# First mixer started on half of the features, and a fixed order of the router chain, in a two-block transformer kernel on one core

## The chip, the core and the metric

The kernel runs on one NeuronCore of a Trainium2 chip. The core has a matrix engine (PE; its weight loads are shown apart, as PEld), a vector engine (DVE), a scalar engine (ACT), a general engine (POOL) and a sequencer that issues most transfers (SP). Each takes its instructions in order and they meet at semaphores. The metric is the device time of one execution in microseconds (us): 730.86 us before, the median of three runs (730.46 to 731.74).

## The reference

One sequence of 256 tokens, 1024 features, everything in float32, goes through two blocks. Only the first block's front and its router are touched by the change:

```
mod = silu(c) @ w_ada + b_ada              # 1024 x 6144, cut into six vectors of 1024
h   = rms_norm(x, g_mix) * (1 + scale_m) + shift_m
x   = x + gate_m * hybrid_mixer(h)         # h @ w_in (1024 x 2896), two attentions, w_out
h   = rms_norm(x, g_ffn) * (1 + scale_f) + shift_f
x   = x + gate_f * hierarchical_moe(h)     # 4 groups of 8 experts, 2 chosen per token
```

The second block (a gated recurrence and a dense feed-forward layer) follows on the same x.

## The kernel before

**Tiles.** A feature index is written on 128 partitions times 8: feature 8p + j lies on partition p, in slice j of a tile. `hTh[:, j]` and `hTl[:, j]` (128 x 256 tokens) are the leading and the remaining bits of slice j of h. A weight is cut in the same way (`split`, `hilo`, lines 85 to 93: ACT copies the high part, `wih`, DVE subtracts it, `wil`), and `mm3` makes three products of a pair. `mm` (line 99) issues every product, so nearly all of PE's rows carry the line L100 and are told apart by their tiles.

**Start.** SP loads four pieces of 1 MB of `w_ada` for the shift (vector 0), then x, then four pieces for the scale (vector 1), then `w_in` columns. `ada(v)` multiplies c's silu (`csr`) with the four pieces into one bank (`p_ada`), ACT copies it (`part`), small products turn it into a column (`p_col`) and DVE adds the bias (`modcol`). x is normed into `xn`, PE turns it (`p_tr`), and `scaled` (line 414) makes `hTh` and `hTl` of all eight slices with the factor `ac` = (1 + scale) g_mix. Only then the projections start: `proj_fm` (line 467) works in four steps of two slices, each of 24 products (`p_w`) into two banks.

**The rest of the mixer.** A string of letters (line 885) names the order of the remaining steps: i, q, b, a are the projections for the index queries, the two query sets and the keys, X and Y the index search on DVE, B to E the attentions. A scheduler places what is not pinned by `tc.keep_in_program_order`; `holding` switches that pinning on, its second entry for PE as well.

**Router.** After the mixer the tokens (two halves, t = 0 and 1) go through `square`, `rstd`, `normed`, `logits`, `groups`, `experts`, `rank`, `places`; `gather_t(t)` (line 998) gathers the tokens of the first four experts by a product of `xn2` with a 0/1 tile `P` (`p_xg`). `gather` (line 1059) scales the result into `xg`, `gate_up` runs the experts (`p_gu`). `cut3` (line 1008) splits `xn2` into three bf16 parts for the gathers of the later units; two of its four steps write `xn2` or read it for the last time (L1011, L1013).

**Buffers.** Weights live in rings: 11 buffers of 1 MB (`raw`), five more in `raw2` and five in `raw3` (`RING`, line 29). `xn2` takes one of the five of `raw3`. SP issues loads in order, so a load that waits for its buffer holds up all behind it. The eight units of four experts follow: unit 0 and the last run straight through, units 1 to 6 each end in a branch (`branch`, line 1302) for an overfull expert, and the loads for the buffers of such a unit are issued behind that branch.

Of the kernel before, what the change touches and what calls it, by code (L numbers as in the profile page):

```python
# [16 lines left out]
T = 256  # L17
D = 1024
# [14 lines left out]
def tile_block(ctx: ExitStack, tc: tile.TileContext, A, out):  # L33
# [87 lines left out]
    act.dma_start(gcol[:, 0], dram("g_mix", 0, [[8, 128], [1, 8]]))  # L121

# [9 lines left out]

    def win_load(c0, n):
        return [load_cols(f"win{c0}_{k}", "w_in", WIN, c0, n, 4 * k, 4) for k in range(2)]

# [29 lines left out]
    small_load(w_bf, dram("w_in", 2888, [[8 * WIN, 128], [WIN, 8], [1, 8]]))  # L165
    small_load(gcol[:, 1], dram("g_ffn", 0, [[8, 128], [1, 8]]))
# [29 lines left out]

    w_iq = win_load(768, 512)
    w_ik = load_cols("wik", "w_in", WIN, 1280, 72, 0, 8)
# [4 lines left out]
    w_bq, w_bk, w_bv, w_aq = [], [], [], []  # L203
    later = {"bq": w_bq, "bk": w_bk, "bv": w_bv, "aq": w_aq}
    for v in (2, 3, 5, 4):
        wada[v] = []
    for name in 'bq bq bk 2 2 bk bv bv 3 aq kv 2 2 3 3 aq 3 4 4 4 4 5 5 5 5'.split():
        if name == "kv":
            w_kv = load_cols("wkv", "w_in", WIN, 512, 256, 0, 8)
        elif name in COLS:  # L210
            c0, n = COLS[name]
            k = len(later[name])
            later[name].append(load_cols(f"win{c0}_{k}", "w_in", WIN, c0, n, 4 * k, 4))
        else:
            ada_piece(int(name))
# [112 lines left out]
    def ada(v):  # L328
# [68 lines left out]

    def transpose_block(src, banks, t):
        for j in range(8):
            pe.transpose(banks[j // 2][:, j % 2, t * 128:t * 128 + 128], src[:, j::8], ident)  # L400

    def transposes(src, by_column=False):

        out_ = [bank([128, 2, T], "p_tr") for _ in range(4)]
        if by_column:
            for j in range(8):
                for t in range(2):
                    pe.transpose(out_[j // 2][:, j % 2, t * 128:t * 128 + 128], src[:, t, j::8], ident)
        else:
            for t in range(2):  # L410
                transpose_block(src[:, t], out_, t)
        return out_

    def scaled(banks, scale, bias, hi, lo, keep):

        for j in range(8):
            p = banks[j // 2][:, j % 2]
            sc = scale[:, j:j + 1]
            if bias is None:
                act.activation(hi[:, j], p, AF.Copy, scale=sc)  # L420
                dve.scalar_tensor_tensor(lo[:, j], p, sc, f32(hi[:, j]), op0=OP.mult, op1=OP.subtract)
            else:
                act.activation(hi[:, j], p, AF.Identity, bias=bias[:, j:j + 1], scale=sc)
                full = keep.tile([128, T], FT, name="full", tag="fin", bufs=3)
                dve.tensor_scalar(full, p, sc, bias[:, j:j + 1], op0=OP.mult, op1=OP.add)
                (dve if j % 2 else pool).tensor_tensor(lo[:, j], full, f32(hi[:, j]), op=OP.subtract)

# [3 lines left out]
    xn = prob1.rearrange("p (t a) b -> p t (a b)", t=2)  # L431
    g0, g1 = ada(0), ada(1)
    for _ in g0:
        pass
# [3 lines left out]
    next(g1)  # L438
    xTb = [bank([128, 2, T], "p_tr") for _ in range(4)]
    for t in range(2):  # L440
        transpose_block(xn[:, t], xTb, t)
        next(g1)
    for _ in g1:
        pass
    ac = small.tile([128, 8], FT, name="ac")
    dve.scalar_tensor_tensor(ac, modcol[:, 1], 1.0, gcol[:, 0], op0=OP.add, op1=OP.mult)

# [384 lines left out]

    st = proj_fm(w_iq, iqT, 1.0)
    c0, m0 = next(st)
    r0_ = c0()
    scaled(xTb, ac, modcol[:, 0], hTh, hTl, a1)
    pend.append(lambda: m0(*r0_))
    def loads1():
# [20 lines left out]
    def router_weights():  # L859
# [3 lines left out]
        for j in range(8):  # L863
# [13 lines left out]

    work = {"i": st, "k": proj_ik(), "q": proj_fm(w_bq, bqT, 0.125), "b": proj_fm(w_bk, bkT, 1.0), "v": proj_bv(),
            "a": proj_fm(w_aq, aqT, 0.125, perm=True), "n": proj_kv(), "o": proj_out(0, obT, obL, rsb),
# [63 lines left out]
    def rstd(t, step):  # L943
# [53 lines left out]

    def gather_t(t):
        for j in range(8):
            mm(xgb[j // 4][:, j % 4], xn2[:, t, j::8], P0f[:, t], t == 0 and j % 4 == 0, t == 1)  # L1000

# [5 lines left out]

    def cut3(src, parts):

        act.activation(parts[0], src, AF.Copy)  # L1010
        dve.tensor_tensor(src, src, parts[0], op=OP.subtract)  # L1011
        act.activation(parts[1], src, AF.Copy)
        dve.tensor_tensor(parts[2], src, parts[1], op=OP.subtract)  # L1013

# [305 lines left out]
    for k, st in enumerate(units):  # L1320
        free = 0 < k < nu - 1
        n = len(st.es)
        gate_up(st, "g")
        if not free:
            load_experts(n)
        gate_up(st, "u")
        if not free:
            load_experts(n)
        silu(st)
        if k == 0:  # L1330
            gate_row_end()
        if k == 3:
            fallback()
# [622 lines left out]
```

## Time and profile before

| | |
|---|---|
| median of three runs | 730.86 us |
| the profiled execution, its own time | 731.0 us |
| its span, first to last instruction | 729.3 us |
| PE busy | 661.0 us (91%) |
| PEld, DVE, ACT busy | 511.3, 400.2, 303.5 us |
| read from HBM | 194.81 MB |

The profile is of one execution; all views below are of it. [...] Three stages can be told apart in the page's slices: the mixer up to about 178 us, where PE is 9 tenths busy, the experts from about 200 to 400 us, where the DMA engines are full and PE is not, and the second block, where PE is full to the end.

### The profile page before, as it was taken

How to read it: one execution, taken by the hardware profiler on the slowest of the kernel's cores; microseconds unless marked ns; L12 is line 12 of the kernel's file. 1: busy time of each engine (PE TensorE's matmuls, PEld its weight loads, DVE VectorE, ACT ScalarE, POOL GpSimd, SP SyncE). 2: the span in 40 equal slices, each digit the busy share in tenths (PEclk: the TensorE clock that was granted, in tenths of full speed). 3: DMA queues.
4: the chain of work that ended last, by engine and by line, in shares of the span. 5: the costliest groups of instructions: out<-in, count | busy, mean ns of one | idle time of the engine just before them, and what ended most of it. 6: DMA issues, size and time to landing. Idle time of an engine off the chain costs nothing. (4 is left out here: it accounts for less than half of the span.)

```text
span 729.3 us, 13242 instructions
## 1 busy us (share of the span) xinstructions
PE 661.0 (91%) x5489; PEld 511.3 (70%) x5489; DVE 400.2 (55%) x753; ACT 303.5 (42%) x505; POOL 46.1 (6%) x71
## 2 busy tenths in 40 slices
PE   4799999999899776898696999999999999999996
PEld 1498787677745524445252499987899999898994
DVE  2367967877653221323312378879576555555555
ACT  1446454754541101101110286775465444444445
POOL 7010000001000000000000153100000000000001
PEclk9899999999899998999987999999999999999998
DMA  9999669996469899998999999633535555550001
GB/s 343 372 381 375 233 262 337 378 420 218 175 273 421 328 417 416 359 423 328 421 421 412 372 364 391 220 117 116 174 116 175 196 200 196 172 202 17 1 1 58
DMA packets 69202, 196.93 MB, mean 270 GB/s; under 512 B 7550, under 2 KB 33219, under 8 KB 57350
## 3 DMA queue, kind: packets, MB, share of 16 engines
q1 hardware_dynamic: 67558, 195.30, 70.8%
q8 instruction: 53, 0.87, 0.5%
q10 hardware_dynamic: 1216, 0.30, 0.2%
q0 software_dynamic: 352, 0.28, 0.1%
q14 instruction: 23, 0.19, 0.1%
HBM read 194.81 MB, written 1.05 MB: 269 GB/s over the span
## 5 line engine op out<-in xcount | busy, mean ns | idle before, releaser
L100 PE MATMUL p_gu<-Xl,wguh 128*128 128x256 f32 x352 | 99.8, 284 | 0.0
L100 PE MATMUL p_gu<-Xh,wgul 128*128 128x256 f32 x352 | 99.3, 283 | 0.0
L100 PE MATMUL p_gu<-Xh,wguh 128*128 128x256 f32 x352 | 98.9, 283 | 0.1
L100 PEld LDWEIGHTS p_gu<-Xl,wguh 128*128 128x128 f32 x352 | 67.5, 192 | 0.5
L100 PEld LDWEIGHTS p_gu<-Xh,wguh 128*128 128x128 f32 x352 | 67.1, 192 | 0.7 <-ACT Xh L1385 0.4
L100 PEld LDWEIGHTS p_gu<-Xh,wgul 128*128 128x128 f32 x352 | 67.4, 192 | 0.3 <-DVE wgul L87 0.2
L100 PE MATMUL p_gu<-eg,xg 128*32 128x256 f32 x576 | 43.9, 434 | 16.6 <-PEq L1302 9.2
L100 PEld LDWEIGHTS p_gu<-eg,xg 128*32 128x32 f32 x576 | 21.1, 123 | 37.9 <-issue 26.8
L87 DVE TENSOR_TENSOR wdnl<-wdn,wdnh 128x1024 fp32r<-128x1024 f32 x22 | 27.0, 1225 | 32.4 <-ACT wdnh L86 32.4
L1155 DVE TENSOR_TENSOR sl<-sl,p_gu 128x256 f32<-128x256 f32 x9 | 3.8, 421 | 71.0 <-ACT sl L1154 71.0
L1154 ACT ACTIVATE sl<-p_gu 128x256 f32<-128x256 f32 x9 | 3.5, 383 | 89.4 <-PE p_gu L100 89.4
L100 PE MATMUL p_w<-hTh,wih 128*128 128x256 f32 x128 | 37.7, 298 | 2.5 <-ACT wih L86 2.5
L87 DVE TENSOR_TENSOR wgul<-wup,wguh 128x1024 fp32r<-128x1024 f32 x22 | 27.0, 1225 | 21.3 <-ACT wguh L86 20.2
L86 ACT ACTIVATE wdnh<-wdn 128x1024 fp32r<-128x1024 f32 x22 | 23.3, 1058 | 36.5 <-PE p_gu L100 35.9
L1072 ACT ACTIVATE xg<-p_xg,modcol,af 128x128 f32<-128x128 f32 x36 | 15.5, 460 | 54.1 <-DVE xg L1074 53.8
L87 DVE TENSOR_TENSOR wgul<-wgt,wguh 128x1024 fp32r<-128x1024 f32 x22 | 26.9, 1225 | 19.8 <-ACT wguh L86 19.8
L100 PE MATMUL p_dn<-ed,aT 128*32 128x512 f32 (+2 forms) x304 | 33.1, 573 | 4.9 <-ACT aT L1162 4.9
L100 PE MATMUL p_w<-Xh,w2h 128*128 128x256 f32 x128 | 37.0, 289 | 0.5 <-ACT w2h L86 0.3
L86 ACT ACTIVATE wguh<-wgt 128x1024 fp32r<-128x1024 f32 x22 | 23.3, 1061 | 33.7 <-PE p_gu L100 18.2
L100 PE MATMUL p_w<-hTl,wih 128*128 128x256 f32 x128 | 37.0, 290 | 0.0
L100 PE MATMUL p_w<-hTh,wil 128*128 128x256 f32 x128 | 36.7, 291 | 0.0
L100 PE MATMUL p_w<-Xh,w2l 128*128 128x256 f32 x128 | 36.1, 284 | 0.6 <-DVE w2l L87 0.6
(624 smaller groups left out, 1591.0 us busy)
## 6 DMA issues: line engine op xcount, KB each, us to landing
eg<-in_w_gate_dram SPq DMA_DIRECT2D x32, 1024.0 KB
eu<-in_w_up_dram SPq DMA_DIRECT2D x32, 1024.0 KB
ed<-in_w_down_dram SPq DMA_DIRECT2D x28, 1024.0 KB
wada<-in_w_ada_dram SPq DMA_DIRECT2D x24, 1024.0 KB
w<-in_w_in_dram SPq DMA_DIRECT2D x11, 1024.0 KB
wgt<-in_w_gate_up_dram SPq DMA_DIRECT2D x11, 1024.0 KB
wup<-in_w_gate_up_dram SPq DMA_DIRECT2D x11, 1024.0 KB
wdn<-in_w_down_dram SPq DMA_DIRECT2D x11, 1024.0 KB
```

The source lines that it names most:

```text
L86: held(act.activation(hi, src, AF.Copy))
L87: held(eng.tensor_tensor(lo, src, f32(hi), op=OP.subtract))
L100: held_pe(pe.matmul(o, lhsT, rhs, start=start, stop=stop, skip_group_check=True))
L1072: act.activation(xg[:, j], b[:, jj], AF.Identity, bias=bf_[:, j:j + 1], scale=af[:, j:j + 1])
L1154: act.activation(st.s[:st.n], st.b[:st.n, 0:256], AF.Silu)
L1155: dve.tensor_tensor(st.s[:st.n], st.s[:st.n], st.b[:st.n, 256:512], op=OP.mult)
```

## The change

It does four things.

1. **Features are numbered anew in the first mixer.** Feature 512h + 4p + j is now slice 4h + j, so the first four slices are the first half of the features. The biases and g_mix are loaded to fit (`bcol` in three transfers instead of one).
2. **The start goes by halves.** Pieces of `w_ada` hold 512 columns: two for the first half of the scale, then x, two for the first half of the shift, the first halves of the i and q weights, and only then the four pieces of the second halves. The class `Cols` takes the place of `ada` for vectors 0 and 1. `w_bf` and `wik` become two transfers each.
3. **The order of both halves is pinned on all engines:** two steps of i and one of q on the first four slices, the columns of the second half, one more step of q, the last four slices.
4. **In the router** `normed` writes `xn2` slice by slice, so that `gather_t` and `cut3` read it in one run, and reads `xt` with the stride instead; `cut3` is pinned behind `gather(0)`; `gather_t(0)` is cut in six and two slices around the second half's `rank`; two fillers on PE (`warm`) go; the pinning reaches over the first unit, and `gate_row_end` (`p_row`) goes behind both of its products.

```diff
-    act.dma_start(bcol, dram("b_ada", 0, [[8, 128], [D, 6], [1, 8]]))
+    act.dma_start(bcol[:, 3:5], dram("b_ada", 3 * D, [[8, 128], [D, 2], [1, 8]]))
+    for v in range(2):
+        act.dma_start(bcol[:, v].rearrange("p (h j) -> p h j", h=2),
+                      dram("b_ada", v * D, [[4, 128], [512, 2], [1, 4]]))
...
+    def load_cols(name, c0, n, k=None):
+        src = [dram("w_in", 512 * WIN * h + c0, [[4 * WIN, 128], [WIN, 4], [1, n]]) for h in range(2)]
+        return load(name, (8, n), *src) if k is None else load(name, (4, n), src[k])
...
-    for _ in range(4):
-        ada_piece(0)
+    ada_half(1, 0)
     tc.keep_in_program_order(nc.sync.dma_start(xt, dram("x", 0, [[D, 128], [128 * D, 2], [1, D]])))
-    for _ in range(4):
-        ada_piece(1)
+    ada_half(0, 0)
+    w_iq = [load_cols("win768_0", 768, 512, 0)]
+    w_bq = [load_cols("win1352_0", 1352, 512, 0)]
+    ada_half(1, 1)
+    ada_half(0, 1)
...
+    class Cols:
+        def __init__(self, v, h):
+            self.v, self.h, self.p = v, h, bank([128, 512], "p_ada")
+        def prod(self, q):
+            for r in range(4):
+                mm(self.p[32 * r:32 * r + 32], csr[:, 4 * q + r, :], wada[self.v, self.h][q][:, r], q == 0, q == 1)
+        def cols(self):
+            self.part = a1.tile([128, 512], FT, name="part", tag="fin", bufs=3)
+            held(act.activation(self.part.rearrange("p (j n) -> p j n", j=4),
+                                self.p.rearrange("p (n j) -> p j n", j=4), AF.Copy))
+        def turn(self):
+            v, hs = self.v, slice(4 * self.h, 4 * self.h + 4)
+            p = bank([128, 4], "p_col")
+            for j in range(4):
+                mm(p[:, j:j + 1], self.part[:, 128 * j:128 * j + 128], sel4, j == 0, True)
+            held(dve.tensor_tensor(modcol[:, v, hs], p, bcol[:, v, hs], op=OP.add))
+            if v:
+                held(dve.scalar_tensor_tensor(ac[:, hs], modcol[:, 1, hs], 1.0, gcol[:, 0, hs],
+                                              op0=OP.add, op1=OP.mult))
...
+    def turn_half(h):
+        xTb.extend(bank([128, 2, T], "p_tr") for _ in range(2))
+        for t in range(2):
+            for j in range(4):
+                held_pe(pe.transpose(xTb[2 * h + j // 2][:, j % 2, t * 128:t * 128 + 128],
+                                     xn[:, t, 512 * h + j:512 * h + 512:4], ident))
...
+    first[1].prod(0)
+    turn_half(0)
+    first[1].prod(1)
+    turn_half(1)
+    first[1].cols()
+    first[1].turn()
+    del holding[:]
...
+    holding += [True, True]
+    run = ahead_of(st)
+    tokens(range(2))
+    run()
+    tokens(range(2, 4))
+    for gen in (st, sq_):
+        ahead_of(gen)()
+    second = [Cols(1, 1), Cols(0, 1)]
+    second[0].prod(0)
+    second[0].prod(1)
+    second[0].cols()
+    run = ahead_of(sq_)
+    second[0].turn()
+    second[1].prod(0)
+    second[1].prod(1)
+    second[1].cols()
+    second[1].turn()
+    tokens(range(4, 6))
+    run()
+    tokens(range(6, 8))
+    del holding[:]
...
-    for c in "iiqikqqFqXFXbbYYbbvYTXXF22XY2XYvvYXYXv2BWBa2aaBYBnB3BC33CCCC3BCanB3C!CR4D45D45D45EH45DDDEoHEoEoDEoDEEESZpppp":
+    for c in "iikqFqXFXbbYYbbvYTXXF22XY2XYvvYXYXv2BWBa2aaBYBnB3BC33CCCC3BCanB3C!CR4D45D45D45EH45DDDEoHEoEoDEoDEEESZpppp":
...
+    xnj = xn2.rearrange("p t (j n) -> p t j n", j=8)
     def normed(t):
-        held(act.activation(xn2[:, t], xt[:, t], AF.Copy, scale=rs2[:, t:t + 1]))
+        held(act.activation(xnj[:, t], xt[:, t].rearrange("p (n j) -> p j n", j=8), AF.Copy,
+                            scale=rs2[:, t:t + 1]))
...
-    gather_t(0)
-    warm(2)
+    gather_t(0, range(6))
     groups(1)
     experts(1)
     rank(1)
+    gather_t(0, range(6, 8))
     places(1)
-    warm(0)
-    gather_t(1)
-    del holding[:]
+    gather_t(1, range(8))
...
     gather(0, xgb)
+    for step in range(2):
+        for t in range(2):
+            cut3(xnj[:, t], [xn3[:, i, t] for i in range(3)], step)
+    del holding[:]
...
+        if k == 0:
+            holding += [True, True]
         gate_up(st, "g")
         if not free:
             load_experts(n)
         gate_up(st, "u")
         if not free:
             load_experts(n)
-        silu(st)
         if k == 0:
             gate_row_end()
+            del holding[:]
+        silu(st)
```

**PE at the start.** `p_ada` are the products with `w_ada`, `p_tr` the turned tokens, `p_col` the columns, `p_w` the projections. PE's rows before:

```order
L100 MATMUL p_ada<-wada_3_101,csr 32x512 x4
L100 MATMUL p_col<-selh,part 64x1 x16
L100 MATMUL p_ada<-wada_0_104,csr 32x512 x4
L400 MATMUL p_tr<-ident,prob_94 128x128 x8
L100 MATMUL p_ada<-wada_1_106,csr 32x512 x4
L400 MATMUL p_tr<-ident,prob_94 128x128 x8
L100 MATMUL p_ada<-wada_2_108,csr 32x512 x4
L100 MATMUL p_ada<-wada_3_110,csr 32x512 x4
L100 MATMUL p_col<-selh,part 64x1 x16
L100 MATMUL p_w<-hTh,wih 128x256
```

And now, the first columns and then, behind 72 products `p_w`, the columns of the second half:

```order
L102 MATMUL p_ada<-wada_0_1_104,csr 32x512 x4
L480 MATMUL p_tr<-ident,prob_96 128x128 x8
L102 MATMUL p_col<-sel_215,part 128x1 x4
L102 MATMUL p_w<-hTh,wih 128x256
...
L102 MATMUL p_ada<-wada_1_0_110,csr 32x512 x4
L102 MATMUL p_ada<-wada_1_1_112,csr 32x512 x4
L102 MATMUL p_col<-sel_215,part 128x1 x4
L102 MATMUL p_ada<-wada_1_0_114,csr 32x512 x4
L102 MATMUL p_ada<-wada_1_1_116,csr 32x512 x4
L102 MATMUL p_col<-sel_215,part 128x1 x4
L102 MATMUL p_w<-hTh,wih 128x256
```

The second half's four pieces, their two copies on ACT and their columns stand between PE's 72nd and 73rd product of the mixer; all columns stood ahead of the first.

**DVE at the start.** `full` is a scaled slice, from which `hTl` is made; `wil` the low part of a weight. Before:

```order
L357 TENSOR_TENSOR modcol<-p_col,bcol 128x8
L446 SCALAR_TENSOR_TENSOR ac<-modcol,gcol 128x8
L425 TENSOR_SCALAR full<-p_tr,ac,modcol 128x256
L87 TENSOR_TENSOR wil<-win_0_119,wih 128x1024
L425 TENSOR_SCALAR full<-p_tr,ac,modcol 128x256 x2
```

And now:

```order
L393 TENSOR_TENSOR modcol<-p_col,bcol 128x4
L89 TENSOR_TENSOR wil<-win_0_106,wih 128x1024
L456 TENSOR_SCALAR full<-p_tr,ac,modcol 128x256 x2
L457 TENSOR_TENSOR hTl<-full,hTh 128x256
L456 TENSOR_SCALAR full<-p_tr,ac,modcol 128x256 x2
```

The first weight's low part has moved ahead of the first slice.

**DVE in the router.** `gone` and `selb` mark the chosen experts of the second half of the tokens, `P` is its 0/1 tile, the rows `xn` belong to `cut3`. Before:

```order
L981 MATCH_REPLACE gone<-top_243,le_1897 128x32
L1011 TENSOR_TENSOR xn_1884<-xn_1884,xn_1910 128x8x128
L982 TENSOR_SCALAR selb<-gone 128x32
L990 SCALAR_TENSOR_TENSOR pos_1902<-p_pos,selb 128x32
L1088 COPY counts<-p_cnt 128x32
L991 TENSOR_TENSOR P_1914<-iota_1898,pos_1902 128x128
```

And now, with the place to which `cut3` has gone:

```order
L1057 MATCH_REPLACE gone<-top_250,le_1899 128x32
L1058 TENSOR_SCALAR selb<-gone 128x32
L1066 SCALAR_TENSOR_TENSOR pos_1904<-p_pos,selb 128x32
L1067 TENSOR_TENSOR P_1916<-iota_1900,pos_1904 128x128
...
L1152 TENSOR_SCALAR xg<-p_xg,af,modcol 128x128
L1189 CAST comb_2060<-crest 128x64
L1190 TENSOR_TENSOR comb_2060<-crest,comb_2060 128x64
L1088 TENSOR_TENSOR xn_1886<-xn_1886,xn_1912 128x1024 x2
L1091 TENSOR_TENSOR xn_1912<-xn_1886,xn_1912 128x1024 x2
```

`selb` follows `gone` at once, and all four steps of `cut3` on DVE stand behind the last `xg` of unit 0.

## Rows read from the trace of the kernel before

**Rows 1.** Windows, all engines: us, PE, PEld, DVE, ACT, POOL, PEclk, DMA share, GB/s.

```profile
190.00:205.50 15.50, 11.93 (x95) 8.38 (x98) 11.18 (x22) 7.97 (x13) 0.00 (x0) 0.89 0.01 1
...
239.00:243.50 4.50, 1.43 (x25) 0.97 (x28) 1.18 (x3) 0.00 (x0) 0.00 (x0) 1.00 0.26 67
243.50:300.00 56.50, 43.01 (x472) 24.97 (x465) 13.83 (x30) 5.04 (x14) 1.02 (x2) 0.88 1.01 415
```

**Rows 2.** Waits of SP's queue, 0 to 215 us: total us, times, longest.

```profile
SPq L252 <- DVE xn L1013: 25.1, 1, 25.1
```

**Rows 3.** Timeline of the start: start us, us, engine, line, operation [idle before <-releaser].

```profile
1.75 0.56 ACTq L121 DMA_DIRECT2D gcol<-in_g_mix_dram  x1
...
4.08 0.89 DVE L324 COPY csr<-cs 128x256 f32<-128x256 f32 x1
...
6.17 1.93 PE L100 MATMUL p_ada<-wada,csr 128*32 128x512 f32 x8 [6.17 <-DMA wada<-in_w_ada_dram]
...
14.47 1.94 PE L100 MATMUL p_ada<-wada,csr 128*32 128x512 f32 x8 [0.64 <-DMA wada<-in_w_ada_dram]
...
17.02 1.06 ACT L395 ACTIVATE prob<-xt 128x1024 f32<-128x1024 f32 x1
...
21.91 0.75 DVE L437 TENSOR_SCALAR prob<-xt,rsr 128x1024 f32<-128x1024 f32 x1
...
21.95 1.94 PE L400 MATMUL p_tr<-ident,prob 128*128 128x128 f32 x8 [0.41 <-DVE rsr L390]
...
26.48 1.06 PE L100 MATMUL p_ada<-wada,csr 128*32 128x512 f32 x8
...
29.22 0.60 ACT L351 ACTIVATE part<-p_ada 128x512 f32<-128x512 f32 x1 [8.22 <-PE p_ada L100]
...
31.02 0.17 DVE L357 TENSOR_TENSOR modcol<-p_col,bcol 128x8 f32<-128x8 f32 x1 [8.36 <-PE p_col L100]
...
33.42 1.23 DVE L87 TENSOR_TENSOR wil<-win,wih 128x1024 fp32r<-128x1024 f32 x1 [0.86 <-ACT wih L86]
...
33.82 0.41 PE L100 MATMUL p_w<-hTl,wih 128*128 128x256 f32 x1
```

**Rows 4.** Windows of the tile p_w alone: us, PE, PEld, DVE, ACT, PEclk, DMA.

```profile
36.00:38.50 2.50, 2.50 (x14) 2.50 (x14) 0.00 (x0) 0.00 (x0) 0.50 1.04 377
40.00:42.00 2.00, 2.00 (x19) 2.00 (x18) 0.00 (x0) 0.00 (x0) 1.00 1.07 383
```

**Rows 5.** Timeline of ACT about 50 us.

```profile
49.94 0.60 ACT L494 ACTIVATE iqT<-p_w 128x512 f32<-128x512 f32 x1 [0.86 <-PE p_w L100]
50.54 1.06 ACT L86 ACTIVATE wih<-win 128x1024 fp32r<-128x1024 f32 x1
```

**Rows 6.** Timeline of PE at 161 us.

```profile
160.79 0.95 PE L100 MATMUL p_ssq<-ones,sq 128*128 128x1 f32 x8
```

**Rows 7.** Timeline of DVE in the router.

```profile
189.49 0.18 DVE L981 MATCH_REPLACE8 gone<-top,le 128x32 f32<-128x32 f32 x1
191.52 2.00 DVE L1011 TENSOR_TENSOR xn<-xn,xn 128x1024 f32<-128x1024 f32 x1 [1.85 <-PE p_xg L100]
193.43 0.18 DVE L982 TENSOR_SCALAR selb<-gone 128x32 bf16<-128x32 f32 x1
...
203.24 2.07 DVE L1013 TENSOR_TENSOR xn<-xn,xn 128x1024 bf16<-128x1024 f32 x1 [1.08 <-ACT xn L1012]
```

**Rows 8.** Timeline of PE in the router.

```profile
186.56 0.91 PE L108 MATMUL p_warm<-ones,ident 128*128 128x128 f32 x6
...
194.54 4.17 PE L100 MATMUL p_xg<-P,xn 128*128 128x128 f32 x16 [0.68 <-DVE P L991]
...
199.84 1.98 PE L100 MATMUL p_row<-modrow,ones 128*128 128x512 f32 x4
...
205.78 3.64 PE L100 MATMUL p_gu<-eu,xg 128*32 128x256 f32 x64
209.35 2.85 PE L100 MATMUL p_xg<-Pq,xn 128*128 128x128 bf16 x48
```

More of the change, by code (lines that the diff above doesn't have):

```diff
@@ L131, in tile_block, with ada_half @@
     WIN = 2896
-    def win_load(c0, n):
-        return [load_cols(f"win{c0}_{k}", "w_in", WIN, c0, n, 4 * k, 4) for k in range(2)]
+    def ada_half(v, h):
+        wada[v, h] = [load(f"wada{v}_{h}_{q}", (4, 512), dram("w_ada", 4 * q * 6 * D + v * D + 512 * h,
+                                                              [[8 * 6 * D, 128], [6 * D, 4], [1, 512]]))
+                      for q in range(2)]
     xt = const.tile([128, 2, D], FT, name="xt")
@@ L164, in tile_block @@
     w_bf = const.tile([128, 8, 8], FT, name="w_bf")
-    small_load(w_bf, dram("w_in", 2888, [[8 * WIN, 128], [WIN, 8], [1, 8]]))
+    for h in range(2):
+        small_load(w_bf[:, 4 * h:4 * h + 4], dram("w_in", 512 * WIN * h + 2888, [[4 * WIN, 128], [WIN, 4], [1, 8]]))
     small_load(gcol[:, 1], dram("g_ffn", 0, [[8, 128], [1, 8]]))
@@ L206, in tile_block @@
         wada[v] = []
-    for name in 'bq bq bk 2 2 bk bv bv 3 aq kv 2 2 3 3 aq 3 4 4 4 4 5 5 5 5'.split():
+    for name in 'bq bk 2 2 bk bv bv 3 aq kv 2 2 3 3 aq 3 4 4 4 4 5 5 5 5'.split():
         if name == "kv":
-            w_kv = load_cols("wkv", "w_in", WIN, 512, 256, 0, 8)
+            w_kv = load_cols("wkv", 512, 256)
         elif name in COLS:
@@ L410, in transposes, with scaled @@
             for t in range(2):
-                transpose_block(src[:, t], out_, t)
-        return out_
-    def scaled(banks, scale, bias, hi, lo, keep):
-        for j in range(8):
+                for j in range(8):
+                    pe.transpose(out_[j // 2][:, j % 2, t * 128:t * 128 + 128], src[:, t, j::8], ident)
+        return out_
+    def scaled(banks, scale, bias, hi, lo, js):
+        for j in js:
             p = banks[j // 2][:, j % 2]
             sc = scale[:, j:j + 1]
[L419 to L426, printed above, removed]
-    xn = prob1.rearrange("p (t a) b -> p t (a b)", t=2)
-    g0, g1 = ada(0), ada(1)
-    for _ in g0:
-        pass
+            held(act.activation(hi[:, j], p, AF.Identity, bias=bias[:, j:j + 1], scale=sc))
+            full = a1.tile([128, T], FT, name="full", tag="fin", bufs=3)
+            held(dve.tensor_scalar(full, p, sc, bias[:, j:j + 1], op0=OP.mult, op1=OP.add))
+            held((dve if j % 2 else pool).tensor_tensor(lo[:, j], full, f32(hi[:, j]), op=OP.subtract))
+    xn = prob1.rearrange("p (t a) b -> p t (a b)", t=2)
+    ac = small.tile([128, 8], FT, name="ac")
+    first = [Cols(1, 0), Cols(0, 0)]
+    holding += [True, True]
+    first[0].prod(0)
+    first[0].prod(1)
+    first[0].cols()
+    first[0].turn()
+    del holding[:]
     for t in range(2):
@@ L437, in tile_block @@
         dve.tensor_scalar(xn[:, t], xt[:, t], r, None, op0=OP.mult)
[L438 to L446, printed above, removed]
+    xTb = []
+    def turn_half(h):
[12 more added lines that the diff above has]
+    del holding[:]
     rsa = const.tile([128, 2], FT, name="rsa")
@@ L831, in flush, with tokens, ahead_of @@
             pend.pop(0)()
[L833 to L837, printed above, removed]
+    st, sq_ = proj_fm(w_iq, iqT, 1.0), proj_fm(w_bq, bqT, 0.125)
+    def tokens(js):
+        scaled(xTb, ac, modcol[:, 0], hTh, hTl, js)
+    def ahead_of(gen):
+        cut, prod = next(gen)
+        r = cut()
+        return lambda: prod(*r)
+    holding += [True, True]
+    run = ahead_of(st)
[18 more added lines that the diff above has]
+    del holding[:]
     def loads1():
@@ L996, in tile_block, with gather_t @@
     xgb = [bank([128, 4, 128], "p_xg") for _ in range(2)]
-    def gather_t(t):
-        for j in range(8):
-            mm(xgb[j // 4][:, j % 4], xn2[:, t, j::8], P0f[:, t], t == 0 and j % 4 == 0, t == 1)
+    def gather_t(t, js):
+        for j in js:
+            mm(xgb[j // 4][:, j % 4], xnj[:, t, j], P0f[:, t], t == 0 and j % 4 == 0, t == 1)
     def gather_mm(u, banks, t):
@@ L1006, in gather_mm, with cut3 @@
                    t == 0 and j % 4 == 0 and i == 0, t == 1 and i == 2)
[L1008 to L1013, printed above, removed]
+    def cut3(src, parts, step):
+        if step == 0:
+            held(act.activation(parts[0], src, AF.Copy))
+            held(dve.tensor_tensor(src, src, parts[0], op=OP.subtract))
+        else:
+            held(act.activation(parts[1], src, AF.Copy))
+            held(dve.tensor_tensor(parts[2], src, parts[1], op=OP.subtract))
     holding += [True, True]
```

33 lines of the change are left out of this document (15 added, 18 removed).

## The prediction

> **What bounds the kernel now.** I read the windows first, then what SP's queue waits for, then the timelines of the two places that change. PE is the bound of the mixer, so a start of its products some time earlier is worth that time there, if PE then keeps its pace. After the mixer the order turns round: from 190.0 to 205.5 us the DMA engines are empty (share 0.01), and from 243.5 on they are full at 415 GB/s while PE has idle time [rows 1]. The reader is to see two things: the empty stretch is paid in full by the stage behind it, and SP stood 25.1 us in one wait, for L1013, the last step of `cut3` on DVE, because `xn2` holds the buffer of the next expert load [rows 2]. There is a second, smaller hole, 239.0 to 243.5 at share 0.26: 3.3 us in which the loads behind unit 1's branch are waited for [rows 1].
>
> **The start.** A piece of 1 MB lands every 2.77 us: the first is used at 6.17, the fourth at 14.47 [rows 3]. Today nine pieces stand ahead of the first product. With the change it is five, so the fifth lands at 6.17 + 4 x 2.77 = 17.3 and the eleventh, the last of the second halves, at 33.9. x now comes third, at 11.7; from the first square (17.02) to the end of the norm (21.91 + 0.75) took 5.6 [rows 3], so `xn` is there at 17.4, no later than that piece. Then on PE: the second four of the first eight transposes, half of 1.94 (18.4), the last `p_ada` group at 1.94 (20.3), eight transposes at 1.94 (22.3), during which ACT's 0.60 copy ends, and the columns. These are now 4 products of one column instead of 16 of 64 rows; the nearest row is `p_ssq`, 8 records in 0.95 [rows 6], so 23.2. From `modcol` to the first product with `hTl` it took 31.02 to 33.82, 2.8 [rows 3]; `ac` leaves that path, `wil` with its 1.23 [rows 3] enters it ahead of `full`. I take 2.8 plus half of 1.23, so 26.6: 7.2 us earlier than 33.82. At the pace of 26.48 (1.06 for a `p_ada` group instead of 1.94 [rows 3]) it would be 1.7 less.
>
> This lead is not kept. [...] Before the low stretch PE had stood mostly idle, waiting for columns and `hTl`. The same idle time now stands before 26.6, so I take the same low stretch, 33.82 to 38.5, 4.7 us or 22 products, and 50 more at 0.12: the 72nd is done at 26.6 + 4.7 + 6.0 = 37.3. There PE turns to the second half's columns, which have landed: twice two groups of 1.06, ACT's 0.60 for which PE must wait, and columns of 0.95, 2 x 3.7 = 7.4, to 44.7. All of that lies on PE's path now, where the same work today lies under the landing of the pieces. The fourth step, 24 x 0.12 = 2.9, covers DVE, ACT and POOL on the second half's tokens; the 96th product is done at 47.6. Today: ACT waits for PE at 49.94 until the first bank is complete, which is the 114th product, so the 96th stands at 49.94 - 18 x 0.12 = 47.8 [rows 5]. From both sides: without any low stretch, 24.9 + 8.6 = 33.5, bounded by the eleventh piece's landing, 43.8, a gain of 4.0; with the columns and the fourth step at the lower clock as well (4 x 0.88 + 1.0 + 24 x 0.09), 54.3, a loss of 6.5. The likeliest row is that of the same low stretch (0.2); half of the low stretch saved would give some 1.2 more. I take a gain of 1.0.
>
> Hidden: ACT issues two transfers more ahead of its first function, 0.56 each; `csr` is done at 4.97, and the first piece lands at 6.17 [rows 3], so 1.1 fits into 1.2. The split `w_bf` and `wik` and the later place of all small loads on SP stand behind full DMA queues (share 1.04 to 1.07 [rows 4]), and their users come after 96 products. If a half piece with its shorter runs lands slower, five pieces at 5% cost 0.7. No wait is added ahead of the later projections: each needs a piece that is queued as early as before.
>
> **The router.** Today DVE starts L1011 at 191.52, after PE has read `xn2`, and `selb`, ready since 189.49 + 0.18, runs only at 193.43. PE's gather of the second half starts 1.1 behind `selb`, at 194.54, and takes 4.17. Three more steps of `cut3` stand between the `xg`, and the u products, which need 3.64, end at 205.78 + 3.64; the gather of unit 1 starts at 209.35 [rows 7, 8].
>
> With the change `selb` runs at 189.7 and the gather starts at 190.8. Its 16 records read a weight tile of stride 8 today, 0.25 each; the fillers of the same shape on an unstrided tile took 0.91 for 6, 0.15 each [rows 8]. The changed `xn2` has the unstrided form, so 16 x 0.15 = 2.4, to 193.2 (bound from above: still 4.17, and 0.5 for the two slices left of the first half, 195.5). The g products start there; they need eight `xg` that no `cut3` step interrupts any more, and take the u group's 3.64 plus some 0.2 of waiting, then u 3.64, then `p_row` 1.98 [rows 8], which has lost the gap that hid it: 193.2 + 0.2 + 7.3 + 2.0 = 202.7, bound 205.0. Against 209.35 that is 6.6 earlier, or 4.4.
>
> What is late next is `cut3` itself: behind the last `xg` at about 196, ACT copies (1.06 [rows 5]) and DVE subtractions (1.23 [rows 3], now that the view is unstrided, against 2.00 [rows 7]) alternate: 1.06 + 4 x 1.23 = 6.0, so 202.0, just ahead of unit 1's gather at 202.7. That is also when SP gets `xn2`'s buffer: 203.24 + 2.07 = 205.3 today, so 3.3 earlier. The DMA queue then runs dry 3.3 earlier, at the hole before 243.5, and is filled again when unit 1 is through, 4.4 to 6.6 earlier; the hole of 3.3 us has room for the difference. Behind it the transfers are full, so what unit 1 gains is kept. I take 6.0, near the upper end, since the fillers' row has the same shape and data type; the low end is 3.3, if only the buffer counts.
>
> [...]
>
> **Sum.** 731.0 (the profiled execution; median 730.86) - 1.0 - 6.0 = 724.0 us.
>
> **Rivals.**
> - *The start pays better.* No low stretch on the first products, as after 38.5, when PE stayed at 1.00 [rows 4]; 3.5 to 4 there and 6 in the router: 721. Against it: PE still waits for columns and `hTl` before 26.6, as it did before 33.82.
> - *Only the buffer counts.* The experts follow SP alone, the gain in the router is 3.3 and the start gives 0.2 to 1: 727. For it: 25.1 us of one wait. Against it: the hole at 239 hangs on unit 1, not on SP's first load.
> - *No change*, 730 to 732: the start loses some 3 (columns at the lower clock) and the router gives 3.3.
> - *Slower.* The stop-and-go start never earns the full clock: 72 products at 0.21 (15.1) from 26.6, columns at 2 x (2 x 1.94 + 0.65 + 1.5) = 12.1, the fourth step 5.1, so the 96th at 58.9 instead of 47.8, 11.1 lost against 6.0 won: 736. It decides from the point where the 96th product comes after 53.8. For it: the clock fell today after the same kind of waiting; against it: it rose again within 4.7 us of products in a row.
>
> [...]
>
> **How the numbers follow.** Both parts as reckoned, 721.8 to 726.5: 0.52. The better start, below that: 0.16. Only the buffer, 726.5 to 729.4: 0.16. Within 0.2% (1.5 us, about what a measurement of this kernel can tell from no change): 0.08. Slower: 0.08. Faster is the first three, 0.84. The range of 719.5 to 729.0 leaves out the last two and the far ends of the second and third.
>
> **What would show it.** Right: the first `p_w` between 24 and 27; a low-clock window there; the second half's `p_ada` near 37; the 96th product 0 to 2 us earlier; `selb` right behind `gone`; gather records of 0.15; unit 1's gather some 7 us earlier, of which 1 is the start's; the empty DMA stretch some 3 us shorter and the hole at 239 nearly gone. Wrong: records of 0.25 in the gather (4.4 instead of 6.0); low clock up to the fourth step; SP still waiting for `cut3` past unit 0's products.

## The result, and the profile after

The changed kernel took 722.0 us (median of four runs, 720.95 to 723.37) where the kernel before took 730.66: a ratio of 0.9878, 95% interval 0.9856 to 0.9900. The forecast was 724.0. In a later set of runs (e11 below) the ratio was 0.9872 (0.9845 to 0.9899). The profiled run has a span of 719.3 us, 10.0 less than before. One of the eight executions of e12 below took 1628 us and is left out of its ratio. The sum came out right; how it is made up did not, and that is what the experiments are about.

**The start.** PE's timeline in the changed kernel:

```profile
7.22 1.93 PE L102 MATMUL p_ada<-wada,csr 128*32 128x512 f32 x8 [7.22 <-DVE csr L337]
...
18.95 1.23 PE L102 MATMUL p_ada<-wada,csr 128*32 128x512 f32 x8
...
24.78 0.38 PE L102 MATMUL p_w<-hTl,wih 128*128 128x256 f32 x1 [1.43 <-POOL hTl L457]
34.90 1.92 PE L102 MATMUL p_ada<-wada,csr 128*32 128x512 f32 x16
...
41.28 1.05 PE L102 MATMUL p_col<-sel,part 128*128 128x1 f32 x8 [0.78 <-ACT part L385]
```

The first product with `hTl` stands at 24.78 instead of 33.82 [rows 3]. The second half's columns lie bare on PE's path from 34.90 to 42.3, 7.4 us, as reckoned. The first product waits for `csr` and is 1.05 us late (7.22 against 6.17): ACT's two extra transfers, which put its first step at 3.79 instead of 2.34, were not hidden. At 18.95 PE was still 0.6 us behind the forecast's 18.4; from there on the last group and the transposes behind it ran in 1.23 each instead of the 1.94 that I had assumed, and 24.78 is earlier than the 26.6 of the forecast.

**The router and SP.** DVE, PE and SP's queue in the changed kernel, the places of [rows 7], [rows 8] and [rows 2]:

```profile
187.34 0.18 DVE L1057 MATCH_REPLACE8 gone<-top,le 128x32 f32<-128x32 f32 x1
187.55 0.18 DVE L1058 TENSOR_SCALAR selb<-gone 128x32 bf16<-128x32 f32 x1
...
196.29 2.36 DVE L1091 TENSOR_TENSOR xn<-xn,xn 128x1024 bf16<-128x1024 f32 x2
```

```profile
188.67 2.02 PE L102 MATMUL p_xg<-P,xn 128*128 128x128 f32 x16
190.62 3.66 PE L102 MATMUL p_gu<-eg,xg 128*32 128x256 f32 x64
194.10 3.64 PE L102 MATMUL p_gu<-eu,xg 128*32 128x256 f32 x64
197.66 1.99 PE L102 MATMUL p_row<-modrow,ones 128*128 128x512 f32 x4
199.48 2.84 PE L102 MATMUL p_xg<-Pq,xn 128*128 128x128 bf16 x48
```

```profile
SPq L263 <- DVE xn L1091: 19.0, 1, 19.0
```

`selb` follows `gone` at once; the 16 gather records take 2.02, 0.13 each instead of 0.25; the gather of unit 1 starts at 199.48 instead of 209.35. SP's wait for `xn2`'s buffer is 19.0 instead of 25.1 us, and it goes on at 198.80 instead of 205.46. The windows show what that does to the DMA engines (last columns: the granted clock of PE as a share of its full one, the PEclk of the rows above; DMA share; GB/s); the hole at 239 to 243.5 [rows 1] is gone:

```profile
190.00:200.00 10.00, 10.00 (x149) 5.84 (x148) 7.80 (x18) 8.20 (x12) 0.00 (x0) 1.00 0.09 15
200.00:205.00 5.00, 4.42 (x70) 3.20 (x71) 1.61 (x5) 2.38 (x7) 0.00 (x0) 1.00 0.91 365
205.00:230.00 25.00, 24.00 (x264) 11.81 (x257) 10.49 (x18) 2.44 (x7) 0.00 (x0) 1.00 1.01 421
230.00:240.00 10.00, 6.36 (x84) 4.06 (x83) 0.56 (x3) 0.00 (x0) 0.00 (x0) 0.83 1.01 415
240.00:250.00 10.00, 9.41 (x141) 5.87 (x132) 2.80 (x7) 2.44 (x7) 0.00 (x0) 1.00 1.01 419
```

### The profile page after: what moved, and what is told of

The parts are those of the page before. It is cut to its first block, busy times and chain, and to the rows that moved or that the text cites. A ratio compares the mean times of both kernels' runs of the same rounds, so it can differ in the third digit from the quotient of the medians.

```text
span 719.3 us, 13181 instructions
## 1 busy us (share of the span) xinstructions
PE 655.8 (91%) x5453; PEld 508.1 (71%) x5453; DVE 397.7 (55%) x757; ACT 303.1 (42%) x507; POOL 47.9 (7%) x71
## 3 DMA queue, kind: packets, MB, share of 16 engines
HBM read 194.81 MB, written 1.05 MB: 272 GB/s over the span
## 4 chain that ended last, share of the span: by engine, by line
PE 40%; DMA 7%; DVE 2%; ACT 1%; POOL 0%; issue 0%; SPq 0%; DVEq 0%; POOLq 0%; ACTq 0%
PE p_gu L102 18%; PE p_acc L102 11%; PE p_w L102 8%; DMA ed<-in_w_down_dram 4%; DMA eu<-in_w_up_dram 3%; PE p_o L102 1%; PE p_sc L102 1%; PE p_gate L102 0%; POOL xt L1873 0%; DVE w2l L89 0%; ACT SS L1876 0%; PE p_row L102 0%; PE p_tr L1467 0%; PE p_dn L102 0%; DVE hs__8967 L1707 0%
## 5 line engine op out<-in xcount | busy, mean ns | idle before, releaser
L102 PE MATMUL p_gu<-eg,xg 128*32 128x256 f32 x576 | 43.0, 428 | 10.3 <-PEq L1383 4.4
L102 PE MATMUL p_dn<-ed,aT 128*32 128x512 f32 (+2 forms) x304 | 35.9, 574 | 5.4 <-ACT aT L1243 5.0
L1149 ACT ACTIVATE xg<-p_xg,modcol,af 128x128 f32<-128x128 f32 x36 | 15.5, 461 | 56.1 <-DVE xg L1152 55.9
```

Of the source, the lines that this page charges most:

```text
L102: held_pe(pe.matmul(o, lhsT, rhs, start=start, stop=stop, skip_group_check=True))
L1149: held(act.activation(xg[:, j], b[:, jj], AF.Identity, bias=bf_[:, j:j + 1], scale=af[:, j:j + 1]))
```

## The experiments

Twelve runs, in three sets of four; each set shares one chip and its own runs of the kernel before, so kernels of different sets are compared by their ratio to it. The table is read from the profiled run of each: where the router's first square starts, where SP passes `xn2`'s buffer (the restart), where unit 1's gather starts, the empty DMA time (one minus the share, summed over windows of 5 us), and PE's idle time ahead of the g products of the experts.

| kernel | ratio (95%) | span | square | restart | gather 1 | empty 210-260 | empty 190-400 | idle before g |
|---|---|---|---|---|---|---|---|---|
| before | 1 | 729.3 | 176.15 | 205.46 | 209.35 | 3.6 | 25.2 | 16.6 |
| changed | 0.9878 (0.9856-0.9900) | 719.3 | 175.59 | 198.80 | 199.48 | 0.0 | 15.8 | 10.3 |
| e1 router only | 0.9939 (0.9917-0.9962) | 722.5 | 176.24 | 199.46 | 200.14 | 1.4 | 17.2 | 15.5 |
| e2 start only | 0.9954 (0.9935-0.9973) | 729.2 | 177.89 | 205.60 | 209.50 | 0.8 | 22.6 | 11.5 |
| e3 old layout | 0.9977 (0.9962-0.9993) | 727.6 | 177.12 | 207.30 | 203.75 | 0.0 | 23.2 | 11.0 |
| e4 old order | 0.9903 (0.9878-0.9927) | 721.8 | 175.45 | 199.16 | 204.33 | 2.1 | 17.5 | 8.3 |
| e5 b_forget early | 1.0082 (1.0054-1.0110) | 735.5 | 186.79 | 212.66 | 213.34 | | | 10.5 |
| e6 ring turned | 0.9829 (0.9805-0.9854) | 718.9 | 177.16 | 195.86 | 201.05 | 2.2 | 13.4 | 9.2 |
| e7 buffer held | 0.9907 (0.9886-0.9928) | 722.6 | 175.90 | 202.96 | 199.78 | 0.0 | 18.9 | 10.4 |
| e8 weights early | 1.0067 (1.0044-1.0090) | 734.6 | 185.94 | 211.89 | 212.57 | | | 10.2 |
| e9 p_lft late | 0.9894 (0.9867-0.9921) | 723.6 | 177.58 | 200.81 | 201.49 | 0.0 | 17.8 | 10.9 |
| e10 p_lft late, ring | 0.9853 (0.9826-0.9881) | 717.8 | 176.12 | 194.82 | 200.01 | 2.1 | 13.1 | 9.0 |
| e11 changed again | 0.9872 (0.9845-0.9899) | 720.2 | 174.51 | 199.31 | 200.00 | 0.0 | 16.8 | 10.5 |
| e12 router only again | 0.9935 (0.9909-0.9960) | 725.3 | 175.87 | 200.67 | 201.35 | 0.8 | 20.7 | 15.8 |

Behind the last product of the experts (`p_sc`, which adds a unit's result to the tokens) 307.8 to 308.1 us are left in all fourteen profiles, so the kernels differ only ahead of it. Span less 190 less the empty time up to 400 is 513.4 to 516.7 in the twelve rows that have all columns: between the router and 400 us, a microsecond in which the DMA engines stood empty was about a microsecond of the total. (e5 and e8, whose mixer ends some 10 us later, give 521.4 and 520.8.)

**e1, e12: the router's part alone**, run twice.

```diff
-            mm(xgb[j // 4][:, j % 4], xn2[:, t, j::8], P0f[:, t], t == 0 and j % 4 == 0, t == 1)
+            mm(xgb[j // 4][:, j % 4], xnj[:, t, j], P0f[:, t], t == 0 and j % 4 == 0, t == 1)
...
```

> The kernel before with only the router's edits: xn2 written feature by feature, cut3 pinned behind the last xg, unit 0 pinned. Theory A (the router alone pays nearly all): unit 1's gather some 9 us earlier than 209.35, since the start's lead at the end of the mixer was only 0.6 us in the changed kernel; time 722.0 to 723.5. Theory B (the router is worth the 6.0 that was forecast and the start the other 2.7): 724.5 to 725.5. Theory C (the two parts need one another): above 726.

> The kernel of the first run again (router's edits alone, the start as before), beside the changed kernel on one chip. Theory A: 0 to 1.5 us above the changed kernel. Theory B: 3 us or more above it.

0.9939 and 0.9935 of 730.7 and 730.14 are 4.5 and 4.7 us less. Theory A of e1 is out, and B's 6.0 lies at the edge of the intervals (2.8 to 6.6 us over both). The median of e1, 726.5, is theory C's number, but not for its reason: alone the two parts give 4.5 and 3.4 us (e2), 7.9 of the 8.9 of both, which is within the intervals. Unit 1's gather came 9.2 earlier in e1 and SP 6.0, so most of unit 1's gain is not paid out.

**e2, e11: the start's part**, alone and as the changed kernel beside e12.

```diff
-    for _ in range(4):
-        ada_piece(0)
+    ada_half(1, 0)
...
```

> The kernel before with only the start's edits, router and experts as before. Theory A: the lead of the start is lost again at the forget gate (p_lft waits some 2.7 us for lf near 63 to 66, and the clock then falls); the first square of the router comes 0 to 1 us earlier, time 729.8 to 731. Theory B: the start carries 2 us or more to the end: 727 to 729. In both, router as before: unit 1's gather 33 us behind the first square.

> The changed kernel itself, beside the next run on one chip, to have the start's worth as a difference of two kernels that share everything else. Theory A (the start is worth what the router's first square shows, 0.6 us): 0 to 1.5 us below the next run. Theory B (it is worth the 3.4 to 4.4 that the medians of the earlier runs give): 3 us or more below it.

Alone it is worth 3.4 us (2.0 to 4.7 by the interval); from e11 and e12, 0.9872 against 0.9935, it is 4.6 us. Theory B in both, and yet theory A's observation stands too: at the router's first square there is, on the mean, nothing of it. Seven profiles with the new start lie at 174.51 to 177.89, three with the old at 175.87 to 176.24. The scatter is the clock's, which stood at 1.00 or at 0.50 (in the kernel before, 0.50 from 32 to 38 us and 1.00 from 40 to 60). PE's busy time from 22 to 176 us, times what the clock lacks of 1.00 in windows of 2 us, is 0.0 us in the profile at 174.51, 3.3 to 3.4 in the three at 175.45 to 175.90, and 4.4 to 4.5 in the three at 177.12 to 177.89. The granted clock in 24 to 32 us of the changed kernel, and of the same kernel in e11, where PE had waited for `hTh` and `hTl` just as long (0.85 and 1.43 or 1.42 us):

```profile
24.00:28.00 4.00, 3.22 (x20) 3.23 (x21) 2.68 (x6) 2.93 (x5) 1.46 (x2) 0.77 1.05 387
28.00:32.00 4.00, 4.00 (x30) 4.00 (x30) 1.99 (x2) 0.50 (x1) 0.00 (x0) 0.80 1.05 385
```

```profile
24.00:28.00 4.00, 2.81 (x23) 2.79 (x23) 2.59 (x6) 2.57 (x5) 1.46 (x2) 1.00 1.05 388
28.00:32.00 4.00, 3.21 (x26) 2.98 (x25) 2.40 (x3) 0.91 (x1) 0.00 (x0) 1.00 1.05 384
```

Most of the start's worth is made elsewhere: of the 5.1 us between the spans of e12 and e11, 1.4 stand at the first square and as much at the restart, the rest arises among the experts. Each of the middle units ends in a conditional branch (`tc.If`, L1302 before, L1311 in e12 and L1383 after). PE behind unit 1 in e12 and in e11 (start us, us, ..., idle before and its releaser):

```profile
227.50 3.70 PE L100 MATMUL p_sc<-yf,PTs 128*128 128x512 f32 x8
235.44 5.35 PE L100 MATMUL p_gu<-eg,xg 128*32 128x256 f32 x64 [4.24 <-DMA ed<-in_w_down_dram]
```

```profile
226.15 3.70 PE L102 MATMUL p_sc<-yf,PTs 128*128 128x512 f32 x8
230.25 0.63 PE L102 MATMUL p_gu<-eg,xg 128*32 128x256 f32 x4 [0.41 <-PEq L1383]
234.49 5.12 PE L102 MATMUL p_gu<-eg,xg 128*32 128x256 f32 x58 [3.61 <-issue]
```

In e12 `p_sc` ends at 231.20, PE goes on 4.24 us later and SP issues its next load at 235.16, 4.0 later. In e11 `p_sc` ends at 229.85, PE begins after 0.41 and stops 3.61 us after four products, but SP, whose queue the DMA engines live on, issues at 229.97, 0.1 later. SP's first load there in e12 and in e11:

```profile
235.16 2.09 SPq L252 DMA_DIRECT2D ed<-in_w_down_dram  x3
```

```profile
229.97 1.28 SPq L263 DMA_DIRECT2D ed<-in_w_down_dram  x3
```

In both, and in the kernel before, SP's load stands 0.28 ahead of PE's first product: the stop at the branch itself held SP as well, the one a few products later did not. Behind unit 5 PE waits 4.20 us in e12, and 1.04 and a little later 2.41 in e11. Behind units 2 and 6 e12 stops a second time some 20 products after the branch, for 2.78 and 2.51 us, where e11 has 0.38 and nothing. The page has the sum in one row (busy, mean ns of one, idle before and its main releaser), of the kernel before and of the changed one:

```profile
L100 PE MATMUL p_gu<-eg,xg 128*32 128x256 f32 x576 | 43.9, 434 | 16.6 <-PEq L1302 9.2
```

```profile
L102 PE MATMUL p_gu<-eg,xg 128*32 128x256 f32 x576 | 43.0, 428 | 10.3 <-PEq L1383 4.4
```

The last column of the table: 15.5 to 16.6 in the three kernels with the old start, 8.3 to 11.5 in the eleven with the new one, e2 among them, whatever the router. So the start's edits, which lie 200 us earlier, go with shorter stops behind the branches. That is no price yet. In e2's own profile, the slowest of its twelve executions, PE idled 5.1 us less there than in the kernel before, but restart and end of the experts stand at 205.60 and 421.1 against 205.46 and 421.4: the hole at 239 is nearly gone, and another, from 300 to 310, is 3.4 us of empty time instead of 1.7. No single profile shows where e2's 3.4 us come from.

What lies in the stops, the traces show. Among the DMA queues is one of the kind "instruction" with 53 packets of 16 KB, and some of them land there. Here is its line (packets, MB, share) for 231.2 to 235.4 us of e12 and for 230.9 to 234.4 us of e11, the two stops above:

```profile
q8 instruction: 1, 0.02, 1.6%
```

```profile
q8 instruction: 1, 0.02, 2.0%
```

The packet lasts from 232.47 to 233.56 in e12 and from 232.00 to 233.09 in e11, and PE goes on 1.9 and 1.4 us behind it. In the fourteen profiles every stop of PE of more than 1.5 us from 205 to 425 us has such a packet landing in it, but for four in which PE waits for `eu`. Together these stops are 26.0 to 30.5 us with the old start and 17.8 to 23.2 with the new one. That PE waits for the packet is my reading: no view names it as what ended a stop. Why the new start shortens the stops is not shown either: e12 and e11 differ by the start alone, in PE's products among others (5485 and 5453), and no run changed the number of instructions ahead of a branch and nothing else.

**e3, e4: layout against order**, each in the changed kernel. e3 has the old layout of `xn2` in the new order, e4 the new layout with `cut3` in its old places.

```diff
-    xnj = xn2.rearrange("p t (j n) -> p t j n", j=8)
+    xnj = xn2.rearrange("p t (n j) -> p t j n", j=8)
...
```

```diff
-    experts(1)
+    experts(1, lambda: cut3(0, 0, True))
...
```

> The changed kernel with xn2 laid out as before (token's features in order, the gather and cut3 read it with a stride of 8), all in the new order. Theory A (stride costs where it is read on the path): 16 records of 0.25 in the second half of the gather instead of 0.12, 2.1 us, cut3's four steps 2.05 instead of 1.0 to 1.2, hidden behind unit 0's products as far as they reach: cut3 ends some 4 us later, about 203, unit 1's gather at 203: 724 to 726. Theory B (cut3 is hidden altogether): 2.1 us, 724. Theory C (the layout is worth nothing on the path, the order all): 722.

> The changed kernel with cut3 in its old places (ACT's copies behind normed, DVE's first subtraction between gone and selb, the others between the xg) and the gather's first half in one piece, but xn2 in the new layout. Theory A (the order is worth more than the layout): selb runs some 2 us behind gone, xg interrupted by three steps of 1.0 to 1.2, unit 1's gather some 4 us later than in the changed kernel: 725 to 727. Theory B (the layout is nearly all, since it shortens every one of these steps): 722 to 723.5.

In the new order the layout is nearly all: without it 1.7 of the 8.9 us are left, and without the order 7.1 (e4's theory B; e3 is dearer than any of its theories). But the two need one another. Beside the start alone (e2, 3.4), the layout is worth 3.7 in the old order and 7.2 in the new one, and the order loses 1.7 with the old layout and wins 1.8 with the new; each of these differences is uncertain by some 2 us. e3's PE and ACT show why; the gather's 16 records and two ACT copies cost twice what they do in the changed kernel (2.02 and 1.99):

```profile
190.91 4.05 PE L102 MATMUL p_xg<-P,xn 128*128 128x128 f32 x16
```

```profile
196.74 4.12 ACT L1086 ACTIVATE xn<-xn 128x1024 bf16<-128x1024 f32 x2
```

`cut3` behind all `xg` with steps of 2.05 ends so late that SP restarts at 207.30, later than before the change, and that is what the time follows: against e2, which shares its start, e3's unit 1 gather is 5.8 us earlier, its restart 1.7 later and its time 1.7 longer. e4 is the other half: its gather is 4.9 later than the changed kernel's, SP's restart 0.4, its time 1.8 (the intervals overlap).

**e7, e6: the buffer by itself.** e7 holds `xn2` for three more reads whose result is not used; e6 turns the ring of buffers so that `xn2`'s comes eight loads later.

```diff
+    for _ in range(3):
+        held(dve.tensor_reduce(q2[:, 1:2], xn2[:, 1], axis=AX.X, op=OP.max))
```

```diff
+RING2 = [1, 1, 2, 2, 1, 1, 1, 1, 3, 1, 2, 1, 1, 2, 2, 1, 1, 3, 3, 3, 3]
...
-            n = RING[i % len(RING)]
+            n = RING[i] if i < 20 else RING2[(i - 20) % len(RING2)]
...
-    load_experts(RING.count(3))
+    load_experts(RING.count(3) - 1)
```

> The changed kernel with three more reads of xn2 on DVE behind cut3 (1.1 us each, their result is not used), which hold its buffer 3.3 us longer and leave the products of units 0 and 1 where they are. Theory A (restart and unit 1's end bound the stage together, so the later restart is paid): the DMA engines stay full behind it, time 724.5 to 725.5. Theory B (unit 1's gather bounds it, and the transfers have room): 722 to 722.5.

> The changed kernel with the ring of weight buffers turned so that xn2's buffer is taken eight loads later: SP's next load waits for unit 0's first g product (about 191.6) and not for cut3 (198.7). Theory A (unit 1's end on PE and the DMA queue's restart bound the stage together): the empty stretch comes back as a hole of some 5 us before SP passes unit 1's branch at 230.7, PE no longer waits 3.6 us for weights there, time 721 to 722. Theory B (the restart alone bounds it): the 7 us are kept, 715 to 717.

In e7 the restart is 4.2 later, with unit 1's gather in its place (199.78), and the span 3.3 longer; by the ratios it is 2.1 us, with intervals that overlap, and the time, 724.86, is theory A's. Half or more of a late restart is paid. In e6 the restart is 2.9 earlier although the mixer ended 1.6 later; theory A's hole is there, but small:

```profile
195.00:200.00 5.00, 5.00 (x82) 2.83 (x75) 4.50 (x4) 4.56 (x5) 0.00 (x0) 1.00 0.63 224
230.00:235.00 5.00, 3.44 (x43) 1.66 (x45) 1.87 (x4) 0.00 (x0) 0.00 (x0) 1.00 0.62 216
```

It gives back 1.9 (0.38 of 5 us) and keeps some 3.6 by the ratios: between A and B. This is the fastest kernel by its ratio. With e9's edit as well (e10, below) it was 3.2 below e9 on the same chip.

**e5, e8, e9, e10: where the start's lead goes in the mixer.** PE waits 2.7 us for `lf` at `p_lft` (the forget gate) in the changed kernel and 1.0 before. e5 loads b_forget earlier, e8 also puts weights ahead of the small loads, e9 puts `p_lft` behind 24 products, e10 is e9 with the turned ring.

```diff
+    bfr = a1.tile([1, 8], FT, name="bfr")
+    small_load(bfr, dram("b_forget", 0, [[8, 1], [1, 8]]))
     rows = a1.tile([64, 128], FT, name="rows")
...
-    bfr = a1.tile([1, 8], FT, name="bfr")
-    small_load(bfr, dram("b_forget", 0, [[8, 1], [1, 8]]))
```

```diff
+    kept_ = list(trickle)
+    del trickle[:]
     w_iq.append(load_cols("win768_1", 768, 512, 1))
+    w_bq.append(load_cols("win1352_1", 1352, 512, 1))
+    trickle.extend(kept_)
     w_ik = load_cols("wik", 1280, 72)
...
```

```diff
-            pe.transpose(p[:, t * 128:t * 128 + 128], lf[:, t], ident)
+            held_pe(pe.transpose(p[:, t * 128:t * 128 + 128], lf[:, t], ident))
...
+        elif c == "[":
+            holding.extend([True, True])
```

The string of steps in e9 has `iikqFqXb[bF]X` where it was `iikqFqXFXbb`.

> The changed kernel with the 32-byte load of b_forget issued right behind gcol's instead of fourteenth, so that p_bfr stands directly behind p_iwt on PE and not 44 products later. Theory A (the start's lead is lost at the forget gate): PE's wait of 2.7 us for lf shrinks to 0 to 1 and the low clock behind it (1.4 to 1.7 us in 66 to 72) goes with it; the router's first square comes about 3 us earlier, 718.5 to 720. Theory B (the lead is lost again at a later wait of the mixer, whatever the gate does): 721.5 to 722.5.

> The kernel of the first run of this set (b_forget early) with the second halves of iq's and bq's weights issued ahead of all small loads and of wik. Theory A (the DMA engines' empty stretch at 36 to 40 us in the changed kernel costs nothing, since PE waits for no load up to the end of the mixer): same time as that kernel within 1 us, though the empty stretch moves or goes. Theory B (what is late there is late everywhere behind it): 2 to 3 us less than that kernel.

> The changed kernel with PE's two transposes of lf (p_lft, the forget gate) put behind 24 products of the next projection instead of ahead of them; the order on the other engines moves only there and in what DVE does between 66 and 100 us. Theory A (part of the start's lead is lost at this wait): PE's 2.7 us of waiting and the 1.4 to 1.7 us of low clock behind it go, the router's first square comes 3 to 4 us earlier than 175.6, time 718 to 719.5. Theory B (what is won there is lost before the router, on another wait): first square as before, 721.5 to 722.5.

> That kernel with the turned ring of the sixth run as well (xn2's buffer taken eight loads later). Theory A (the two gains lie in different stages and add): 3 us below the run before this one, 714.5 to 716.5. Theory B (an earlier router only makes the hole ahead of unit 1's branch larger): within 1 us of the run before this one.

e5 missed: 6 us slower than the kernel before. Its wait at `p_lft` did shrink, to 0.9, but the scheduler moved other work at 95 to 112 us, and DVE then stood for PE:

```profile
112.48 0.69 DVE L808 COPY bPT<-p_pt 128x512 f32<-128x512 f32 x1 [10.65 <-PE p_pt L804]
```

So e5 doesn't answer its question. e8 has the same fault; against e5 it is 1.2 us less, and its empty stretch only moved to 40-42 us (share 0.63): nothing of theory B's 2 to 3, and nothing firm for A. e9 keeps the order elsewhere and answers it: theory B, with a time 1.6 us above e11's by the ratios (the intervals overlap). The wait shrinks to 0.6, the clock stays at 1.00 behind it (from 60 to 174 us in e10), and the first square is no earlier (177.58, and 176.12 in e10, against 174.51 in e11). New waits stand at 80 to 100 us. DVE is busy for 10.00 of 10 us from 80 on, in e10 as in e11, and PE's longest wait there (1.34 us) is for DVE, so DVE is likely the bound. The windows of e10:

```profile
80.00:90.00 10.00, 8.66 (x40) 5.83 (x40) 10.00 (x48) 2.85 (x5) 0.00 (x0) 1.00 0.43 149
```

e10 is theory A's for the ring (3.2 less than e9), though not its time, since e9's part gave nothing.

## Why the prediction was right, and where it was not

- *The start, 1.0.* The first `p_w` (24.78, forecast 24 to 27), the bare columns (7.4) and the low clock in the first profile were as reckoned. The 0.21 and 0.12 us for a product are read from [rows 4], 12 whole records in 2.5 us at a granted clock of 0.50 and 17 in 2.0 at 1.00; in the changed kernel the products follow one another at 0.21 from 26.2 to 29.6 and at 0.12 from there on. The 96th product ended near 45 instead of 47.6, so better than forecast; the router's first square came 0.6 earlier, in e11 1.4 earlier than in e12. But the low stretch is no property of the kernel (e11 has none), and "no wait is added" failed: PE's wait for `lf` grew from 1.0 to 2.7 us, though without it the square came no earlier (e9, e10). Most of what the start is worth, 3.4 to 4.6, arises among the experts and goes with shorter stops behind their branches, which no step of the prediction looked at. Right in sign, wrong in cause, too small by some 3.
- *The router, 6.0.* Measured 4.5 and 4.7, too large by 1.4. Its mechanism was put the wrong way round: "what unit 1 gains is kept" failed. Unit 1's gather came 9.9 earlier instead of 6.6, and e3 and e4 show that the time doesn't follow it. It follows SP's restart; "3.3 earlier" was the term mis-sized. It was 6.7, of which some 4.5 are the router's edits.
- *Why the restart came so early.* I had the last `xg` at 196; `cut3` began at 192.87. `gone` stood at 187.34 instead of 189.49. Of these 2.15 us 0.6 are the start's and 1.6 are no work of the change: PE's clock fell in the profiled run of before (rows below), and from the first square to the second `gone` it took 13.3 there and 11.8 in e2, which has the same router and no such dip; in e11 and e12, which have the new router and such a dip (0.50 to 0.87 in windows from 180 to 186 us), it is 13.3 again. So the restart's 6.7 are 0.6 of the start, 1.6 of the clock and 4.5 of the router's edits. e12 bears this out: its dip is that of the kernel before, it restarts 4.8 earlier, and it is 4.7 faster. The gather took 2.02 instead of 2.4; `cut3` itself took 5.8 (forecast 6.0). The windows of the kernel before (clock: third column from the end):

```profile
182.00:184.00 2.00, 2.00 (x12) 2.00 (x11) 1.76 (x10) 2.00 (x4) 0.00 (x0) 0.51 0.98 414
184.00:186.00 2.00, 2.00 (x15) 2.00 (x13) 0.30 (x2) 1.97 (x2) 0.00 (x0) 0.64 1.04 438
```

- *The hole at 239.* Taken as room that unit 1's lead would fill. It was the branch: behind unit 1's last product, at 239.13, SP stood 2.8 and PE 3.1 us before they went on, with an instruction packet from 239.29 to 240.38 in between.
- *The rivals.* "Only the buffer counts" had the mechanism, with the wrong size. "The start pays better" had the size, not its reason. "Slower" didn't come: the clock was at 1.00 from 30 to 60 us in the changed kernel, and the pages of e2 to e4, e6, e7 and e9 to e11 show nine tenths or more from 36 to 54 us.
- *The stride.* At a stride of eight floats against none, PE took 0.25 against 0.13 per record of the gather and ACT 2.06 against 1.00 per copy of `cut3` (e3 and the changed kernel), DVE 2.00 to 2.07 [rows 7] against 1.18 per subtraction. `normed`, which now reads so, took 2.14 instead of 1.14; from the first square to the second `gone` it is 11.8 all the same, as in e2, where `normed` reads without the stride. No run has another stride, so where the price begins is not shown.

Two errors of opposite sign, some 3 too little at the start and 1.4 too much in the router, left 724.0 near 722.0. That the sum fits so well is luck.

## What to carry to other kernels

Where a stage lives on transfers, add up the time in which the DMA engines stand empty and ask which instruction frees the buffer that SP waits for; a compute step that came 5.8 us earlier was worth nothing where that one came 1.7 later (e3). Before ordering work anew, look for reads with a wide stride: here the layout of one tile brought the steps of three engines from 0.25 to 0.13, from 2.06 to 1.00 and from some 2.05 to 1.18 us, and without it the new order lost time. A small change in a kernel with branches is to be measured with the rest kept, and in more than one execution: the stops behind the branches were shorter with edits that lie 200 us ahead of them, and the clock alone moved the router's first square by up to 3.4 us, and its chain by 1.6, from one profile to another.

## What was not expected of the hardware

- PE's idle time ahead of the experts' g products was 15.5 to 16.6 us in three kernels and 8.3 to 11.5 in eleven that differ from them 200 us earlier; behind one branch it was 4.24 in e12 and 0.41 in e11, followed by 3.61 after four products.
- These stops held a packet of 16 KB on the instruction queue; it took some 1.1 us, and PE went on 1.3 to 2.0 us after it had landed (3.0 to 3.4 in the one stop inside unit 3).
- The clock in the start fell in one profile of the changed kernel (0.77 and 0.80 in 24 to 32 us) and not in another (1.00 in e11), with the same instructions.
- Two small loads of `w_bf` and two of `wik` held SP's queue for 5.71 and 4.21 us, and the DMA engines then stood at a share of 0.65 in 36 to 40 us.
